# Adding the two terms of the rounded weights in one 512-column matmul, in the block products that share an accumulator

## The chip, the cores and the metric

The kernel runs on one core of a Trainium2 chip. The metric is the device time of one execution in microseconds; lower is better. A core has PE (the matrix engine, whose weight loads are listed as PEld), DVE (the vector engine), ACT (the scalar engine), POOL and SP. Each takes its own instructions in the order in which they were issued, and waits on the others by semaphores.

## The reference, cut to what matters

One decoder layer over 512 positions of width 1024, in float32: an FFN, a mixer, a second FFN, and a final norm.

```python
def swiglu(x, w_gate, w_up, w_down):
    return (jax.nn.silu(x @ w_gate) * (x @ w_up)) @ w_down
...
x = x + 0.5 * swiglu(rmsnorm(x, ffn1_norm[l]), ffn1_wg[l], ffn1_wu[l], ffn1_wd[l])
x = x + hybrid_mixer(rmsnorm(x, mix_norm[l]), ...)
x = x + 0.5 * swiglu(rmsnorm(x, ffn2_norm[l]), ffn2_wg[l], ffn2_wu[l], ffn2_wd[l])
return rmsnorm(x, final_norm)
```

The change lies in `x @ w_gate` and `x @ w_up` of both FFNs (`D_MODEL` 1024, `D_FF` 2816, so 22 tiles of 128 output rows for each of the two matrices).

## The kernel before, in words

**Split operands.** Every float32 matrix is split into a rounded part and the rest (`wh` and `wl` for weights; ACT rounds, DVE subtracts), and a product is made of three matmuls: rounded weight by rounded data, rounded weight by the data's rest, and the weight's rest by rounded data.

**`ffn_up`.** The first tiles go through plain products (`direct`). From tile `f0` (6 in the first FFN, 4 in the second) on, two tiles n and n+1 of one matrix are computed together by block products: the two weight tiles, each cut into two halves of 512 columns (H), and the data, cut into two halves of 256 positions, form a 2 by 2 block matrix product, which is done with seven products in place of eight. Sums and differences of the data blocks are made once (`moving_operands`); a data block `m` is a tile of 512 columns whose left half (`lo`) holds the rounded 256 columns and whose right half (`hi`) holds their rest. The sums of weight blocks (`s1` to `s4`) are made partly by adding DMAs of POOL, partly on DVE (`add_weights`).

**A pass** is one pair of tiles of one matrix: even passes `w` are the gate, odd ones the up matrix (`o.j = w % 2`). There are 16 passes in the first FFN and 18 in the second. In `stream` the products of a pass stand in the order 1, 2, 4 (of the pass before), 6, 3 (of the pass before), 5, 7. In the first pass there is no pass before, so its order is 1, 2, 6, 5, 7; the last pass ends with 6, 5, 7, 3 (of the pass before), 4, 3.

**A product** (`products`) has four column blocks of three matmuls of 256 columns each: rounded weights by `m[:, lo]`, rounded weights by `m[:, hi]`, rest of the weights by `m[:, lo]`. All three add into the left half of one accumulator of 512 columns. Products 1, 6, 7 and 4 of a pass share one accumulator, `o.beta` (a tile `mm`), in that order: each is read before the next adds to it. Product 2 has its own (`o.p2`) and 5 and 3 share `o.gamma` (both tiles `aux`).

**Reading** (`results`). After 1, 6 and 7 ACT copies the left half of `beta` out, into `t1` or `t2` (tiles `tg` in even passes, `tu` in odd ones). After 4 ACT applies Silu straight from `beta` in an even pass, and in an odd pass DVE multiplies `beta` with the gate. DVE adds what came from `p2` and `gamma`.

**Order.** The stretch is scheduled by hand (`manual_schedule`): one turn of the loop issues the matmuls of product i, the results of product i-1, and `prepare(i + LEAD)` with LEAD = 4: the weight sums due, ACT's rounding `wh` and DVE's rest `wl` of the product four places ahead. The split weights have three buffers of two products each. With `i % 14 == 12` and `i // 14 < f0` a turn also splits one tile of the FFN's hidden values (`halve`: ACT `hh`, DVE `hl`) for the down projection.

Of the kernel before, what the change touches and what calls it, by code (L numbers as in the profile page):

```python
# [11 lines left out]
AF = mybir.ActivationFunctionType  # L12
# [5 lines left out]
KD = D // P  # L18
# [162 lines left out]
def hybrid_kernel(ctx, tc, xt, vec, w1u, w1d, wm, wki, wrg, watt, wrnn, wout, w2u, w2d, both):  # L181
    nc = tc.nc

    out = both[0].rearrange("(k p c) -> k p c", k=KD, p=P)
    turned_out = both[1].rearrange("(j p c) -> j p c", j=2, p=P)
    plan = Plan()
    V, A = plan.engine("DVE", nc.vector), plan.engine("ACT", nc.scalar)
    G, T = plan.engine("POOL", nc.gpsimd), plan.engine("PE", nc.tensor)
# [21 lines left out]
    def slot(dt=F32, name="s"):  # L210
        return plan.take("slot", big.tile([P, S], dt, tag="slot", name=nm(name)))

    def work(name="t", cols=S):
        return plan.take("tmp", tmp.tile([P, cols], F32, tag="tmp", name=nm(name)))

    def awork(name="a"):
        return patt.tile([P, S], F32, tag="att", name=nm(name))

    def psum(tag="mm"):
        return psp.tile([P, S], F32, tag=tag, name=nm(tag))  # L220
# [26 lines left out]
    def wload(src, cols):  # L247
        r, h, l = wtiles(cols)
        Q.dma_start(r, src)
        wsplit(r, h, l)  # L250
        return h, l
# [69 lines left out]
    lo, hi = slice(0, HS), slice(HS, S)  # L321
# [62 lines left out]
    def ffn_up(y, wu, n0, hs, g, waiting=(), given=()):  # L384
# [10 lines left out]
        ws = []  # L395
# [65 lines left out]
        w = count - 1  # L461
# [26 lines left out]
        def products(i):  # L488
            p, w = stream[i]
            o = ws[w]  # L490
            if p == 1:
                o.beta = psum("mm")
            elif p == 2:
                o.p2 = psum("aux")
            elif p == 5:
                o.gamma = psum("aux")
            acc_ = {2: lambda: o.p2, 5: lambda: o.gamma, 3: lambda: o.gamma}.get(p, lambda: o.beta)()[:, lo]
            h, l = (t[:, i % 2 * H:(i % 2 + 1) * H] for t in units[i // 2])
            starts, opens = p in (1, 2, 5), dict(skip_group_check=p not in (1, 2, 5))
            for j in range(KD // 2):  # L500
                c = slice(j * P, (j + 1) * P)
                m = moving[{1: "n11", 2: "b21", 6: "t2", 5: "t1", 7: "r", 4: "q", 3: "n22"}[p]][j]
                T.matmul(acc_, h[:, c], m[:, lo], start=starts and j == 0, stop=False, **opens)
                T.matmul(acc_, h[:, c], m[:, hi], start=False, stop=False, **opens)
                T.matmul(acc_, l[:, c], m[:, lo], start=False, stop=j == KD // 2 - 1, **opens)

        def results(i):
            p, w = stream[i]
            o = ws[w]
            if p == 1:  # L510
                o.t1, o.t2 = (work("tg"), work("tg")) if o.j == 0 else (awork("tu"), awork("tu"))
                A.activation(o.t1[:, lo], o.beta[:, lo], AF.Copy)
            elif p == 2:
                V.tensor_sub(o.t1[:, lo], o.p2[:, lo], o.t1[:, lo])
            elif p == 6:
                A.activation(o.t1[:, hi], o.beta[:, lo], AF.Copy)
            elif p == 7:
                A.activation(o.t2[:, hi], o.beta[:, lo], AF.Copy)
                V.tensor_add(o.t2[:, hi], o.gamma[:, lo], o.t2[:, hi])
                if o.j:  # L520
                    o.h2 = slot(F32, "h")
                    V.tensor_mul(o.h2[:, hi], o.t2[:, hi], ws[w - 1].t2[:, hi])
                else:
                    A.activation(o.t2[:, hi], o.t2[:, hi], AF.Silu)
            elif p == 4:
                if o.j:
                    V.tensor_mul(o.h2[:, lo], o.beta[:, lo], ws[w - 1].t2[:, lo])
                else:
                    A.activation(o.t2[:, lo], o.beta[:, lo], AF.Silu)
            elif p == 3:  # L530
                V.scalar_tensor_tensor(o.t1[:, hi], o.gamma[:, lo], -1.0, o.t1[:, hi], op0=ALU.mult, op1=ALU.subtract)
                if o.j:
                    o.h1 = slot(F32, "h")
                    V.tensor_mul(o.h1, o.t1, ws[w - 1].t1)
                    hs.extend((o.h1, o.h2))
                else:
                    A.activation(o.t1, o.t1, AF.Silu)

        with tc.manual_schedule(engines=ENGINES):
# [32 lines left out]
            for i in range(len(stream)):  # L572
                products(i)
                if i:
                    results(i - 1)
                else:
                    together(results_direct(len(direct) - 1))
                if i + LEAD < len(stream):
                    prepare(i + LEAD)
                else:  # L580
                    halve(hs, f0 + i + LEAD - len(stream))
                if i % 14 == 12 and i // 14 < f0:
                    halve(hs, i // 14)
                if i % 7 == 1 and len(ws) < count:
                    load_ = load(len(ws))
                next(load_, None)
            results(len(stream) - 1)

    def halve(hs, n):
# [45 lines left out]
    for k in range(KD):  # L635
        if k:
            Q.dma_start(x[k], xt[k])
        if k % CH == 0:
            c = slice(k * P, (k + CH) * P)
# [8 lines left out]
    def given(r):  # L648
        h, l = (wsp.tile([P, WMAX], F32R, tag=t, name=nm(t)) for t in ("wh", "wl"))
        wsplit(r, h, l)  # L650
        return h, l

    y = []
    for k in range(KD):
        y.append(norm_tile(k, V_G1, False))
        if k % CH == 0:
            c = slice(k * P, (k + CH) * P)
# [4 lines left out]
    pu, w = psum(), given(AH[0])  # L662
# [672 lines left out]
    po, ws = psum(), []  # L1335
    for a, b in CHUNKS:
        w = wload(w2d[n, :, a * P:b * P], (b - a) * P)
# [42 lines left out]
    o = []  # L1380
# [84 lines left out]
```

## Time and profile before

| | us |
|---|---|
| three runs: 1092.8, 1093.52, 1094.61; median | 1093.52 |
| the profiled execution, its own time | 1094.6 |
| span of the profiled execution, first to last instruction | 1092.5 |
| block products of the first FFN, in the trace | about 74 to 235 |
| block products of the second FFN, in the trace | about 781 to 961 |

The profile is of one execution. Times are microseconds unless marked ns. The page gives each engine's busy time and instructions, and the costliest groups of instructions as line, engine, operation, result and operands by their names in the program, shape, count, busy time, mean duration in ns and idle time before them. Since all engine calls go through one helper, they all show its line, L175; the names tell them apart. `mm<-cm,wh` is a matmul of data block and rounded weights into `mm`, `wl<-s,wh` the rest of a weight sum. The chain of waits follows the work that ended last, in order of time, as start, length, what and count. The table by stage gives each engine's busy time and instruction count in a stretch. The timelines give start, length, engine, operation and count, and in brackets how long the engine had been idle and who released it. DVE's and ACT's lengths include a tail over which the next operation can start already.

### The profile page before, as it was taken

Reading aid. Unit: us, or ns where it says so; the run is one execution under the profiler, and the core shown is the slowest. Engines: PE = TensorE matmul, PEld = TensorE weight load, DVE = VectorE, ACT = ScalarE, POOL = GpSimd, SP = SyncE. Lnnn points to the kernel's source line nnn. Section 1 sums busy time; section 2 is a strip of 40 time slices with the busy share of each in tenths; the row PEclk is TensorE's granted clock in tenths of the full one; section 3 lists DMA queues with packets and bytes.
Section 4 is the critical chain, followed back from the end, with each engine's and each line's share of the span. In section 5 each row is a group of like instructions: output and inputs, shape, how many; then the busy total and the mean of one; then the engine's idle time right before and its main releaser. Section 6 shows DMA issues by size and latency. Waiting matters only on the chain.

```text
span 1092.5 us, 16466 instructions
## 1 busy us (share of the span) xinstructions
PE 1081.0 (99%) x6210; PEld 950.2 (87%) x6210; DVE 761.8 (70%) x1374; ACT 605.1 (55%) x1102; POOL 93.9 (9%) x115
## 2 busy tenths in 40 slices
PE   9999999999999999999999999999999999999997
PEld 7889999998888777888888888888899999988887
DVE  6687877785333778998899867666877777773233
ACT  6565655573222558969785564345655555562222
POOL 0151111100000000000000000002511111000000
PEclk9999999999999999999999999999999999999999
DMA  7396777733333442223232213435977777443322
GB/s 271 72 249 191 186 167 191 169 106 89 105 89 103 116 136 75 79 95 100 71 104 77 78 29 88 134 96 133 243 175 190 191 163 188 116 124 88 106 73 77
DMA packets 60607, 140.22 MB, mean 128 GB/s; under 512 B 7152, under 2 KB 15472, under 8 KB 60528
## 3 DMA queue, kind: packets, MB, share of 16 engines
q1 hardware_dynamic: 45264, 116.31, 33.9%
q0 software_dynamic: 14976, 22.55, 13.6%
q8 instruction: 48, 0.79, 0.3%
q10 hardware_dynamic: 288, 0.31, 0.1%
q14 instruction: 31, 0.25, 0.1%
HBM read 130.24 MB, written 2.10 MB: 121 GB/s over the span
## 4 chain that ended last, share of the span: by engine, by line
PE 87%; DVE 6%; ACT 4%; DMA 2%; issue 1%; SPq 0%; DVEq 0%; ACTq 0%; POOLq 0%
PE mm L175 58%; PE aux L175 29%; DVE wl L175 2%; ACT wh L175 1%; DMA gr<-wrg 1%; DVE yl L175 1%; DMA cm<-cb 1%; ACT L175 1%; DVE yf L175 0%; DMA x<-xt 0%; DVE ca L175 0%; ACT rl L175 0%; DVE h L175 0%; DVE xc L175 0%; ACT yh L175 0%
## 5 line engine op out<-in xcount | busy, mean ns | idle before, releaser
L175 DVE TENSOR_TENSOR wl<-wr,wh 128x1024 fp32r<-128x1024 f32 (+3 forms) x204 | 194.4, 956 | 149.0 <-ACT wh L175 148.4
L175 ACT ACTIVATE wh<-wr 128x1024 fp32r<-128x1024 f32 (+4 forms) x206 | 171.1, 835 | 173.2 <-PE mm L175 73.8
L175 PE MATMUL mm<-cm,wh 128*128 128x256 f32 x1088 | 199.0, 283 | 0.0
L175 PEld LDWEIGHTS mm<-cm,wh 128*128 128x128 f32 x1088 | 169.8, 192 | 0.2
L175 PE MATMUL mm<-yh,wh 128*128 128x512 f32 (+1 forms) x416 | 164.9, 397 | 1.3 <-ACT yh L175 0.7
L175 PE MATMUL mm<-yl,wh 128*128 128x512 f32 (+1 forms) x416 | 163.2, 393 | 0.9 <-DVE yl L175 0.8
L175 PE MATMUL mm<-yh,wl 128*128 128x512 f32 x408 | 160.0, 392 | 0.0
L175 PE MATMUL mm<-cm,wl 128*128 128x256 f32 x544 | 153.9, 283 | 0.0
L175 PE MATMUL aux<-cm,wh 128*128 128x256 f32 x816 | 150.3, 283 | 0.1
L175 PEld LDWEIGHTS aux<-cm,wh 128*128 128x128 f32 x816 | 127.4, 192 | 0.3 <-DMA cm<-cb 0.3
L175 PE MATMUL aux<-cm,wl 128*128 128x256 f32 x408 | 115.5, 283 | 0.0
L175 DVE TENSOR_TENSOR wl<-s,wh 128x512 fp32r<-128x512 f32 x136 | 93.3, 687 | 23.4 <-ACT wh L175 21.6
L175 ACT ACTIVATE wh<-s 128x512 fp32r<-128x512 f32 x136 | 83.0, 623 | 39.0 <-DVE s L175 30.9
L175 PEld LDWEIGHTS mm<-cm,wl 128*128 128x128 f32 x544 | 104.4, 192 | 0.0
L175 PEld LDWEIGHTS mm<-yh,wh 128*128 128x128 f32 (+1 forms) x416 | 78.4, 189 | 19.5 <-ACT yh L175 1.9
L175 PEld LDWEIGHTS mm<-yl,wh 128*128 128x128 f32 (+1 forms) x416 | 78.0, 187 | 17.3 <-DVE yl L175 2.2
L175 PEld LDWEIGHTS mm<-yh,wl 128*128 128x128 f32 x408 | 76.9, 189 | 16.6 <-DVE wl L175 0.3
L175 PE MATMUL mm<-hh,wh 128*128 128x512 f32 (+1 forms) x210 | 79.4, 378 | 0.0
L175 PE MATMUL mm<-hl,wh 128*128 128x512 f32 (+1 forms) x210 | 79.3, 377 | 0.0
L175 PE MATMUL mm<-hh,wl 128*128 128x512 f32 (+1 forms) x210 | 79.1, 377 | 0.0
L175 PEld LDWEIGHTS aux<-cm,wl 128*128 128x128 f32 x408 | 78.3, 192 | 0.0
L175 PE MATMUL aux<-hh,wh 128*128 128x512 f32 x154 | 59.9, 389 | 0.0
(220 smaller groups left out, 1898.6 us busy)
## 6 DMA issues: line engine op xcount, KB each, us to landing
wr<-wm SPq DMA_DIRECT2D x39, 512.0 KB, 3.6
wr<-w2u SPq DMA_DIRECT2D x26, 512.0 KB, 3.9
wr<-w1u SPq DMA_DIRECT2D x21, 512.0 KB, 5.5
s<-w2u SPq DMA_DIRECT2D x36, 256.0 KB, 4.7
s<-w2u POOLq DMA_DIRECT2D x36, 256.0 KB, 5.1
s<-w1u SPq DMA_DIRECT2D x32, 256.0 KB, 5.8
s<-w1u POOLq DMA_DIRECT2D x32, 256.0 KB, 5.5
wr<-w1d SPq DMA_DIRECT2D x16, 448.0 KB, 3.3
```

What stands on the lines that cost most here:

```text
L175: return call(*args, **kw)
```

## The change

In the products that go into `beta`, the two matmuls of the rounded weights, by `m[:, lo]` and by `m[:, hi]`, become one matmul of 512 columns, by the whole of `m`, into the whole accumulator: its left half takes the first term and its right half the second. The third matmul adds into the left half as before. In the last column block the order is turned, so that the wide matmul is last. When the accumulator is read, `whole` copies the right half with ACT and then adds the left half to the copy with DVE. Where ACT (Silu) or DVE (the product with the gate) read `beta` directly after product 4, `whole` now comes first, into `t2`. Products 2, 5 and 3 are as before.

```diff
-            acc_ = {2: lambda: o.p2, 5: lambda: o.gamma, 3: lambda: o.gamma}.get(p, lambda: o.beta)()[:, lo]
+            acc_ = {2: lambda: o.p2, 5: lambda: o.gamma, 3: lambda: o.gamma}.get(p, lambda: o.beta)()
...
-                T.matmul(acc_, h[:, c], m[:, lo], start=starts and j == 0, stop=False, **opens)
-                T.matmul(acc_, h[:, c], m[:, hi], start=False, stop=False, **opens)
-                T.matmul(acc_, l[:, c], m[:, lo], start=False, stop=j == KD // 2 - 1, **opens)
+                if acc_ is o.beta:
+
+                    wide = lambda: T.matmul(acc_, h[:, c], m, start=starts and j == 0, stop=j == KD // 2 - 1, **opens)
+                    rest = lambda: T.matmul(acc_[:, lo], l[:, c], m[:, lo], start=False, stop=False, **opens)
+                    for half in (wide, rest) if j < KD // 2 - 1 else (rest, wide):
+                        half()
+                    continue
+                T.matmul(acc_[:, lo], h[:, c], m[:, lo], start=starts and j == 0, stop=False, **opens)
+                T.matmul(acc_[:, lo], h[:, c], m[:, hi], start=False, stop=False, **opens)
+                T.matmul(acc_[:, lo], l[:, c], m[:, lo], start=False, stop=j == KD // 2 - 1, **opens)
+
+        def whole(out, acc_):
+            A.activation(out, acc_[:, hi], AF.Copy)
+            V.tensor_add(out, acc_[:, lo], out)
...
-                A.activation(o.t1[:, lo], o.beta[:, lo], AF.Copy)
+                whole(o.t1[:, lo], o.beta)
...
-                A.activation(o.t1[:, hi], o.beta[:, lo], AF.Copy)
+                whole(o.t1[:, hi], o.beta)
             elif p == 7:
-                A.activation(o.t2[:, hi], o.beta[:, lo], AF.Copy)
+                whole(o.t2[:, hi], o.beta)
                 V.tensor_add(o.t2[:, hi], o.gamma[:, lo], o.t2[:, hi])
...
             elif p == 4:
+                whole(o.t2[:, lo], o.beta)
                 if o.j:
-                    V.tensor_mul(o.h2[:, lo], o.beta[:, lo], ws[w - 1].t2[:, lo])
+                    V.tensor_mul(o.h2[:, lo], o.t2[:, lo], ws[w - 1].t2[:, lo])
                 else:
-                    A.activation(o.t2[:, lo], o.beta[:, lo], AF.Silu)
+                    A.activation(o.t2[:, lo], o.t2[:, lo], AF.Silu)
```

## The prediction

> **What bounds the kernel now.** I read the page first, then the chain of waits in order of time, then the table by stage, then the timelines of DVE and ACT. The page:
>
> ```profile
> span 1092.5 us, 16466 instructions
> PE 1081.0 (99%) x6210; PEld 950.2 (87%) x6210; DVE 761.8 (70%) x1374; ACT 605.1 (55%) x1102; POOL 93.9 (9%) x115
> L175 PE MATMUL mm<-cm,wh 128*128 128x256 f32 x1088 | 199.0, 283 | 0.0
> ```
>
> PE is at work for 99% of the span, and the matmuls that the change touches have no idle time ahead of them. Their 283 ns overlap, so the price of one is read from the chain, where the piece lengths are start to start:
>
> ```profile
> 173.66 1.44 PE aux L175 x12
> 175.10 2.88 PE mm L175 x24
> ...
> 280.48 14.96 PE aux L175 x66
> ```
>
> Twelve 256-column matmuls take 1.44 us: 120.0 ns each, and a block product 1.44 us. Sixty-six 512-column ones take 14.96 us: 226.7 ns each. The third view is a stage: one pair of passes (14 products, 20.16 us) in the first FFN.
>
> ```profile
> core 0: us, PE busy (x) PEld busy (x) DVE busy (x) ACT busy (x) POOL busy (x), PEclk, DMA share, GB/s
> 177.86:198.02 20.16, 20.16 (x170) 20.16 (x170) 15.52 (x28) 11.64 (x24) 3.50 (x4) 1.00 0.78 195
> ```
>
> PE sets the pace and DVE, with 28 operations and 15.52 us, looks as if it had 4.6 us to spare. How much of that is real depends on the waits inside it, so I need the timeline of DVE in that pair:
>
> ```profile
> 180.01 0.69 DVE L175 TENSOR_TENSOR h<-tu,tg 128x512 f32<-128x512 f32 x1
> ...
> 183.03 0.42 DVE L175 TENSOR_TENSOR tg<-aux,tg 128x256 f32<-128x256 f32 x1
> 184.45 1.48 DVE L175 TENSOR_TENSOR wl<-s,wh 128x512 fp32r<-128x512 f32 x2 [1.00 <-ACT wh L175]
> ...
> 187.59 0.69 DVE L175 TENSOR_TENSOR wl<-wr,wh 128x512 fp32r<-128x512 f32 x1 [0.73 <-ACT wh L175]
> ...
> 189.64 0.42 DVE L175 SCALAR_TENSOR_TENSOR tg<-aux,tg 128x256 f32<-128x256 f32 x1
> 189.97 0.68 DVE L175 TENSOR_TENSOR s<-s,wr 128x512 f32<-128x512 f32 x1
> 191.28 0.69 DVE L175 TENSOR_TENSOR wl<-a,wh 128x512 fp32r<-128x512 f32 x1 [0.62 <-ACT wh L175]
> ...
> 193.09 0.42 DVE L175 TENSOR_TENSOR tu<-aux,tu 128x256 f32<-128x256 f32 x1
> 193.54 0.43 DVE L175 TENSOR_TENSOR h<-tu,tg 128x256 f32<-128x256 f32 x1
> 193.88 0.69 DVE L175 TENSOR_TENSOR wl<-s,wh 128x512 fp32r<-128x512 f32 x1
> 194.49 0.69 DVE L175 TENSOR_TENSOR hl<-h,hh 128x512 fp32r<-128x512 f32 x1
> ```
>
> and the two places of ACT behind its waits:
>
> ```profile
> 183.48 0.42 ACT L175 ACTIVATE tg<-tg 128x256 f32<-128x256 f32 x1 [0.76 <-DVE tg L175]
> 183.80 0.61 ACT L175 ACTIVATE wh<-s 128x512 fp32r<-128x512 f32 x1
> ...
> 186.66 0.38 ACT L175 ACTIVATE tg<-mm 128x256 f32<-128x256 f32 x1 [0.93 <-PE mm L175]
> 186.94 0.62 ACT L175 ACTIVATE wh<-wr 128x512 fp32r<-128x512 f32 x1
> ```
>
> From these rows DVE has four prices. A 512-column step: from 180.01 to 183.03 there are five, 0.604 each. A 256-column step: 193.54 to 193.88, 0.33 to 0.34. The same step when the next operation reads its result: 193.09 to 193.54, 0.45. And a hand-off over ACT, when a DVE result goes to Silu, behind which the next rounding `wh` is queued, on which DVE's next `wl` waits: 183.03 to 184.45, 1.42, that is 1.09 over the step itself.
>
> **The matmuls.** The accumulator `beta` takes 4 of a pass's 7 products, each of four column blocks. In each block two matmuls of 256 columns (240.0 ns) become one of 512 (226.7): 13.3 ns saved. With 34 passes (16 and 18) that is 544 times, 7.25 us, or 0.43 us in a pair, whose PE time falls from 20.16 to 19.73. A page differs: the Trainium skill, "TensorE: Matmul & The Clock Gate", section "Wait — 56ns, not 53.3ns?", gives a warm matmul a fixed cost of about 2.5 ns over its columns. By that rule the whole saving would be an estimated 544 x 2.5 ns = 1.4 us. The trace speaks against it here (120.0 and 226.7 ns for 256 and 512 columns leave a fixed 13.3), so I keep 7.25.
>
> **The halves to be added.** `whole` copies the upper half on ACT and adds the lower one on DVE, for four products of a pass. The copy replaces one that was there, except for product 4, where it is new: 34 copies more on ACT and 136 additions more on DVE. The nearest rows:
>
> ```profile
> L175 DVE TENSOR_TENSOR h<-mm,tg 128x256 f32<-128x256 f32 x17 | 7.2, 424 | 1.1 <-PE mm L175 0.8
> L175 ACT ACTIVATE tu<-mm 128x256 f32<-128x256 f32 x51 | 19.2, 377 | 20.0 <-PE mm L175 20.0
> ```
>
> The same kind of operands, 424 ns, so a step of 0.33 (0.45 where the next operation reads it). ACT, busy 11.64 of 20.16, hides its copy.
>
> DVE's own loop over a pair, if PE never held it up: 20 steps of 512 (14 `wl`, 4 `s`, one `h`, one `hl`) at 0.604, 12.08; 8 of 256, 2.64; two of these read at once by the next, 0.24; one hand-off through the gate's Silu behind product 7, 1.09; the other Silu, 189.64 to 191.28, 1.64 with a step of 0.33 and one of 0.60 inside, so 0.71. Sum 16.76, 3.4 less than PE's time. The change adds 8 steps (2.64), three of them read at once by the next (0.36), and a second hand-off: product 4 of an even pass goes straight from `beta` to Silu today (186.66); now DVE's addition stands in front, so ACT's Silu and the `wh` behind it wait for DVE as at 183.03, 1.09. Together 4.09: **20.85 us for DVE against 19.73 for PE**. The average busy time hid that: a hand-off is idle time that nothing else fills, since DVE takes its operations in order.
>
> **Why PE then waits.** Product 6 adds into the bank that product 1's reader has to leave, and 7 and 4 follow likewise. The reader was ACT, alone; now DVE must have made its addition. From the end of product 1, PE has products 2 and 4 as cover, 2.83 us. In the DVE queue the addition stands behind the `wl` of a product four places ahead, so DVE's lag lands on PE. Release to PE costs little:
>
> ```profile
> 8.22 0.76 DVE yl L175
> 8.98 0.04 issue
> 9.03 12.57 PE mm L175 x54
> ```
>
> Once the lag has grown to 2.83 us PE runs at DVE's 20.85. Only pairs in which `halve` adds its `hl` (194.49) have that sum, by its condition (`i // 14 < f0`, 6 and 4) six in the first FFN and four in the second; the others are 0.60 shorter, 20.25. Against 20.16 before: +0.7 in 8 pairs (5.6; the first pair of each FFN has still to build the lag, and keeps its gain, -0.9) and +0.1 in 7 pairs (0.7).
>
> **The two ends of each stream.** In the first pass only one product lies between 1 and 6. The timelines of DVE and of PE there, in both FFNs:
>
> ```profile
> 77.12 0.68 DVE L175 TENSOR_TENSOR wl<-s,wh 128x512 fp32r<-128x512 f32 x1
> 77.72 0.69 DVE L175 TENSOR_TENSOR wl<-wr,wh 128x512 fp32r<-128x512 f32 x1
> 783.60 0.68 DVE L175 TENSOR_TENSOR wl<-wr,wh 128x512 fp32r<-128x512 f32 x1
> ```
>
> ```profile
> 76.93 0.50 PE L175 MATMUL mm<-cm,wh 128*128 128x256 f32 x2
> 783.66 0.39 PE L175 MATMUL mm<-cm,wh 128*128 128x256 f32 x2
> ```
>
> The addition goes between those two `wl`: 77.72 to 78.14, and product 6, which began at 76.93, at 78.18: 1.25 late. In the second FFN 783.60 to 784.02, so 784.06 for 783.66: 0.4. In the last pass product 7 follows 6 after one product. From the addition of 1 to that of 6, DVE has 0.33 + 0.60 + 0.60 + 0.33 + 0.60 + 0.33 + the hand-off with an `s` inside (1.09) + 0.60 = 4.5, PE 2.83 of cover: up to 1.65 late, of which I take 1.4, since PE itself comes a little late there; twice, 2.8.
>
> **Sum.** 5.6 - 0.9 + 0.7 + 1.65 + 2.8 = 9.9. The steps read 0.60 to 0.604 and 0.33 to 0.34, and where the lag shrinks in the seven short pairs PE gets a part of its 0.43 back; I take 9.0. The profiled execution took 1094.6 us (span 1092.5 and 2.1 around it), 1.1 above the median of 1093.5, so 1103.6 for a like execution, **1102.5** for the median. For the range: the hand-offs fully hidden and the others (rival one) at the lower end; each new addition at 0.45 instead of 0.33 at the upper.
>
> **Rivals.** *DVE keeps up*, and it ends faster: at product 4 the Silu and the `wh` behind it are early enough not to hold DVE. Then the loop is 19.76 in long pairs, PE's time, and 19.16 in short ones. The gain of 7.25 shows, less 1.65 and some 1.0 at the ends: -4.6, a median of 1089. For it: ACT is idle 42% of that stage. Against it: the 0.73 at 187.59 shows DVE waiting on that same `wh` already. It decides at the point where a loop falls under 19.73. Chance 0.12. *A draw*: half of that hand-off is hidden, the loops are 20.3 and 19.7; +1 or so, 1094. Chance 0.12. *All additions at the dependent price*: 0.12 more for the other five of a pair, 0.6 in 15 pairs, 9 us more: 1111. Chance 0.12. *The wide matmul saves nothing*: the weights are loaded once less, but 512 columns could cost 240 ns between 256-column ones, which no row shows mixed. As DVE sets the pace this costs only the first pairs' 0.9: 1103.5. Chance 0.05. My forecast keeps 0.59.
>
> A measurement of this kernel can tell about 0.2%, 2.2 us, from no change. Faster by more: 0.12; within: 0.12; slower: 0.76. The range of 1092.5 to 1109 leaves out the first rival and most of the third.
>
> **What would show it.** In the profile after: `mm<-cm,wh` at 128x512 x544 with some 227 ns a piece in the chain; PE matmuls on `mm` that wait for DVE `tg` and `tu`, some 34 times, 0.2 to 0.9 us each, at product 6; pairs of about 20.8 and 20.2 us instead of 20.16; DVE without idle but at the hand-offs, with over 18 us busy in a pair. It is wrong if PE shows no such waits, or if the pairs are 19.73.

## The result and the profile after

The changed kernel takes 1105.23 us (median of four runs, 1104.55 to 1105.73), the kernel before 1093.72: a ratio of 1.0105, interval 1.0087 to 1.0122, or 11.5 us slower. The forecast was 1102.5, from 1092.5 to 1109. The profiled execution took 1104.55 us.

The page of the kernel after, the lines that answer to those shown of before:

```profile
span 1102.8 us, 15526 instructions
PE 1083.1 (98%) x5666; PEld 919.0 (83%) x5666; DVE 805.0 (73%) x1510; ACT 610.8 (55%) x1136; POOL 93.9 (9%) x115
L175 PE MATMUL mm<-cm,wh 128*128 128x512 f32 x544 | 200.1, 403 | 8.0 <-DVE tg L175 5.3
```

544 matmuls are gone, and ahead of the 544 wide ones there are now 8.0 us of idle time, where there were 0.0. The view of waits, of PE alone (who waits for whom: us in total, times, longest):

```profile
PE mm L175 <- DVE tg L175: 5.3, 9, 1.1
PE mm L175 <- DVE tu L175: 2.6, 2, 1.3
```

Nine and two waits stand there; those of the odd passes, of a tenth of a microsecond each, are too short for it. One of the nine, in the timeline of PE:

```profile
179.15 0.40 PE L175 MATMUL mm<-cm,wh 128*128 128x512 f32 x1
180.07 0.49 PE L175 MATMUL mm<-cm,wh 128*128 128x512 f32 x1 [0.52 <-DVE tg L175]
180.40 0.28 PE L175 MATMUL mm<-cm,wl 128*128 128x256 f32 x1
180.52 0.40 PE L175 MATMUL mm<-cm,wh 128*128 128x512 f32 x1
180.75 0.28 PE L175 MATMUL mm<-cm,wl 128*128 128x256 f32 x1
```

At 179.15 the last matmul of product 4 begins, at 180.07 product 6. From 180.52 on a wide matmul holds PE for 0.23 us, so without a wait product 6 would have begun at 179.38: it is 0.69 us late. The table by stage, one long pair (with a `hl`) and one short pair:

```profile
179.25:200.10 20.85, 20.33 (x138) 18.39 (x136) 18.05 (x37) 11.89 (x26) 3.52 (x4) 1.00 0.72 178
890.30:910.60 20.30, 20.30 (x139) 18.39 (x137) 17.50 (x36) 11.44 (x25) 3.51 (x4) 1.00 0.72 172
```

DVE is busy 18.05 us of a long pair, where it was 15.52. What the other 2.8 us of the pair (20.85 - 18.05) are is shown by its timeline, over the same pair:

```profile
179.60 0.42 DVE L175 TENSOR_TENSOR tg<-mm,tg 128x256 f32<-128x256 f32 x1
179.93 0.68 DVE L175 TENSOR_TENSOR wl<-s,wh 128x512 fp32r<-128x512 f32 x1
...
187.26 0.41 DVE L175 TENSOR_TENSOR tg<-mm,tg 128x256 f32<-128x256 f32 x1
187.71 0.42 DVE L175 TENSOR_TENSOR tg<-aux,tg 128x256 f32<-128x256 f32 x1
189.14 0.69 DVE L175 TENSOR_TENSOR wl<-s,wh 128x512 fp32r<-128x512 f32 x1 [1.00 <-ACT wh L175]
...
191.61 0.41 DVE L175 TENSOR_TENSOR tg<-mm,tg 128x256 f32<-128x256 f32 x1
193.03 0.69 DVE L175 TENSOR_TENSOR wl<-wr,wh 128x512 fp32r<-128x512 f32 x1 [1.01 <-ACT wh L175]
...
194.58 0.42 DVE L175 SCALAR_TENSOR_TENSOR tg<-aux,tg 128x256 f32<-128x256 f32 x1
194.91 0.68 DVE L175 TENSOR_TENSOR s<-s,wr 128x512 f32<-128x512 f32 x1
196.21 0.69 DVE L175 TENSOR_TENSOR wl<-a,wh 128x512 fp32r<-128x512 f32 x1 [0.62 <-ACT wh L175]
...
199.88 0.68 DVE L175 TENSOR_TENSOR hl<-h,hh 128x512 fp32r<-128x512 f32 x1
200.49 0.42 DVE L175 TENSOR_TENSOR tg<-mm,tg 128x256 f32<-128x256 f32 x1
```

From the addition of product 1 (179.60, on which PE's 180.07 waits) to the next of its kind (200.49) it is 20.89 us. Between them DVE stops three times, each time for ACT's `wh`: at 189.14 (behind product 7), at 193.03 (behind product 4, new) and at 196.21 (behind 3). The middle one, in ACT's timeline:

```profile
190.32 0.37 ACT L175 ACTIVATE tg<-mm 128x256 f32<-128x256 f32 x1
192.06 0.42 ACT L175 ACTIVATE tg<-tg 128x256 f32<-128x256 f32 x1 [1.38 <-DVE tg L175]
192.39 0.61 ACT L175 ACTIVATE wh<-wr 128x512 fp32r<-128x512 f32 x1
```

ACT has copied its half by 190.69 and waits until 192.06 for DVE's addition (191.61 to 192.02); then come Silu, `wh`, and DVE's `wl` at 193.03.

### The profile page after: what moved, and what is told of

Same layout as the page of the kernel before. It is cut to its first block, busy times and chain, and to the rows that moved or that the text cites. A ratio compares the mean times of both kernels' runs of the same rounds, so it can differ in the third digit from the quotient of the medians.

```text
span 1102.8 us, 15526 instructions
## 1 busy us (share of the span) xinstructions
PE 1083.1 (98%) x5666; PEld 919.0 (83%) x5666; DVE 805.0 (73%) x1510; ACT 610.8 (55%) x1136; POOL 93.9 (9%) x115
## 4 chain that ended last, share of the span: by engine, by line
PE 75%; DVE 15%; ACT 4%; issue 3%; DMA 2%; SPq 0%; DVEq 0%; ACTq 0%
PE mm L175 52%; PE aux L175 24%; DVE wl L175 6%; ACT wh L175 3%; DVE tg L175 2%; DVE s L175 2%; DVE tu L175 1%; DVE h L175 1%; DMA gr<-wrg 1%; DVE yl L175 1%; DVE yf L175 0%; DVE hl L175 0%; DMA wr<-w1u 0%; DVE ca L175 0%; DMA x<-xt 0%
## 5 line engine op out<-in xcount | busy, mean ns | idle before, releaser
L175 PE MATMUL mm<-cm,wh 128*128 128x512 f32 x544 | 200.1, 403 | 8.0 <-DVE tg L175 5.3
L175 PEld LDWEIGHTS aux<-cm,wh 128*128 128x128 f32 x816 | 131.2, 190 | 3.9 <-DMA cm<-cb 0.4
L175 PE MATMUL mm<-cm,wl 128*128 128x256 f32 x544 | 130.7, 281 | 0.0
L175 PEld LDWEIGHTS mm<-cm,wh 128*128 128x128 f32 x544 | 100.0, 188 | 29.2 <-DVE tg L175 10.3
L175 ACT ACTIVATE tg<-tg 128x256 f32<-128x256 f32 (+1 forms) x61 | 31.2, 512 | 67.6 <-DVE tg L175 67.5
```

The source lines that it names most:

```text
L175: return call(*args, **kw)
```

## The experiments

Two theories stood against each other. The first: a loop of DVE and ACT sets the pace of the block products, made of 8 additions and a hand-off more in a pair, and PE waits for it at product 6. The rivals: the wide matmul saves nothing or costs time itself; DVE's additions alone are too much, whatever the order. All runs are given beside runs of the kernel before on the same chip. "Streams" are the two stretches of block products, from the start of the first to the start of the last of their matmuls in the timeline of PE: 161.60 and 181.32 us before, 167.84 and 185.78 after, together 10.7 us longer. The whole span grew by 10.3.

**The wide matmul alone.** The results are read as in the kernel before.

```diff
-            whole(o.t1[:, lo], o.beta)
+            A.activation(o.t1[:, lo], o.beta[:, lo], AF.Copy)
... (and so in products 6, 7 and 4)
```

> The wide matmul as in the change, but the accumulator is read as in the kernel before: ACT or DVE reads its left half alone, and the right half (the rounded weights by the data's rest, in four of seven products) is left out of the result. Theory (DVE's loop sets the pace, the wide matmul saves 13.3 ns of PE each): DVE is back at 16.8 us a pair, PE at 19.73, so no waits on DVE and the full 544 x 13.3 ns: 1093.7 - 7.2 = 1086.5 us, ratio to before 0.993. Rival (the wide matmul saves nothing, 512 columns between narrow ones cost 240 ns): 1093.7 us, pairs of 20.16 us.

Measured: 1087.68 us against 1093.25, ratio 0.9951 (0.9938 to 0.9963); streams 159.33 and 178.67. So the wide matmul does save: 5.6 us by the medians, 4.9 us in the two streams (338.0 instead of 342.9). Both are less than 7.2. The chain of waits of this run, in order of time:

```profile
103.33 2.81 PE mm L175 x16
106.15 2.88 PE aux L175 x24
...
123.20 2.82 PE mm L175 x16
```

Two products for the shared accumulator take 2.815 us, 352 ns for a wide and a narrow matmul, where the forecast had 226.7 + 120.0 = 346.7 and three narrow ones had 360. A pair is 123.20 - 103.33 = 19.87 us, not 19.73.

**The additions alone.** Three narrow matmuls, of which the one by `m[:, hi]` goes to the right half.

```diff
-                    wide = lambda: T.matmul(acc_, h[:, c], m, ...)
+                    T.matmul(acc_[:, lo], h[:, c], m[:, lo], ...)
+                    T.matmul(acc_[:, lo], l[:, c], m[:, lo], ...)
+                    T.matmul(acc_[:, hi], h[:, c], m[:, hi], ...)
```

> The opposite part alone: three matmuls of 256 columns as before, but the data's rest goes to the right half of the accumulator, so the halves are added when it is read, as in the change. Theory: DVE's loop is that of the change, 20.85 us in a long pair and 20.25 in a short one, and PE's own 20.16 lies under both, so the time is that of the change but for the few places where PE itself was the bound (some 1 us): 1105 to 1107 us. Rival one (the wide matmul, or its turned order in the last block, is what costs): 1094 to 1097 us. Rival two (PE's saving and the waits simply add up): 1105.2 + 7.2 = 1112.5 us.

Measured: 1105.25 us, ratio 1.0111 (1.0096 to 1.0127), streams 168.06 and 185.93; the change has 1.0105 and 167.84 and 185.78. With all of PE's saving taken away the time is the same. That is what it means that another engine sets the pace, and both rivals of this run fall: the wide matmul isn't what costs, and PE's saving and the waits don't add up. PE's waits in this run:

```profile
PE mm L175 <- DVE tg L175: 5.0, 10, 1.5
PE mm L175 <- DVE tu L175: 2.2, 2, 1.1
```

In sum they are a little less than in the change (5.3 and 2.6): PE's own matmuls take longer here (360 ns where the wide and the narrow one take 352), so it comes later and waits less for the same DVE.

**One Silu moved.** The Silu after product 4 is issued behind `prepare(i + LEAD)`.

```diff
-                    A.activation(o.t2[:, lo], o.t2[:, lo], AF.Silu)
+                    late.append(lambda: A.activation(o.t2[:, lo], o.t2[:, lo], AF.Silu))
...
+                while late:
+                    late.pop(0)()
```

> The change, with one instruction moved: the Silu after product 4 of an even pass is issued behind the rounding of the weights four places ahead, instead of ahead of it. Theory (the hand-off over ACT at product 4, 1.09 us of a pair, is part of the loop): long pairs fall from 20.87 to about PE's 19.8, short ones to 19.73; with starts and ends as they are, 1092 to 1095 us. Rival (the volume of DVE's work alone, 8 additions more in a pair, is what costs): no change, 1105 us.

Measured: 1096.36 us, ratio 1.0030 (1.0018 to 1.0041). Not one operation less on DVE, and most of the loss is gone, so it isn't the volume of DVE's work alone. But it is 1.4 us above the upper end of what I expected. The timeline of ACT, then of DVE:

```profile
168.68 0.42 ACT L175 ACTIVATE tg<-tg 128x256 f32<-128x256 f32 x1 [0.85 <-DVE tg L175]
169.00 0.37 ACT L175 ACTIVATE tu<-mm 128x256 f32<-128x256 f32 x1
169.27 0.62 ACT L175 ACTIVATE wh<-wr 128x512 fp32r<-128x512 f32 x1
```

```profile
165.75 0.69 DVE L175 TENSOR_TENSOR wl<-s,wh 128x512 fp32r<-128x512 f32 x1 [1.00 <-ACT wh L175]
...
168.56 0.68 DVE L175 TENSOR_TENSOR wl<-wr,wh 128x512 fp32r<-128x512 f32 x1
169.40 0.42 DVE L175 TENSOR_TENSOR tu<-mm,tu 128x256 f32<-128x256 f32 x1 [0.16 <-ACT tu L175]
169.92 0.69 DVE L175 TENSOR_TENSOR wl<-wr,wh 128x512 fp32r<-128x512 f32 x1
...
172.17 0.69 DVE L175 TENSOR_TENSOR wl<-a,wh 128x512 fp32r<-128x512 f32 x1 [0.62 <-ACT wh L175]
...
185.99 0.69 DVE L175 TENSOR_TENSOR wl<-s,wh 128x512 fp32r<-128x512 f32 x1 [1.00 <-ACT wh L175]
```

The late Silu still waits for DVE (0.85 idle), and now ACT's copy of the next product and its `wh` stand behind it. DVE's addition begins at 169.40 instead of 169.16 (0.60 after 168.56), its `wl` 0.52 after that instead of 0.33: 0.43 of the 1.09 came back. The loop is 185.99 - 165.75 = 20.24 us where the sum gave 20.85 - 1.09 = 19.76, still over PE's 19.87. The hand-offs behind products 7 and 3 are left (1.00 us idle at 165.75, 0.62 at 172.17).

**All three Silus moved,** in the same way.

> The change, with all three Silus of an even pass (after products 4, 7 and 3) issued behind the rounding of the weights four places ahead. Theory: the loop of DVE has no hand-offs left, 20.85 - 1.09 - 1.09 - 0.71 = 18.0 us in a long pair, under PE's 19.73, so pairs of 19.73 us and the gain of 7.2 us less the starts (1.5 us) and part of the ends (2.9 us): 1088 to 1091 us. Rival (volume of DVE's work): no better than with the one Silu moved.

Measured: 1090.26 us, ratio 0.9972 (0.9963 to 0.9982), 3 us under the kernel before; streams 160.59 and 179.24. The stage of one pair, and PE's waits for DVE in the whole run:

```profile
120.87:140.74 19.87, 19.87 (x138) 18.43 (x137) 18.56 (x38) 12.61 (x26) 3.51 (x4) 1.00 0.71 177
```

```profile
PE mm L175 <- DVE tg L175: 1.5, 2, 1.1
```

DVE is now busy 18.56 of 19.87 us, more than in the change, and PE has no idle time: the pair is as long as with the wide matmul alone. The two waits left are those at the start of each stream; the ones at the ends are gone as well.

**The control:** the same move in the kernel before.

> A control: the kernel before, with its three Silus of an even pass issued behind the rounding of the weights, as in the run with all three moved. Theory (before, PE sets the pace and DVE's loop of 16.8 us has slack, so hand-offs cost nothing there): no change, 1093.7 us, pairs of 20.16 us. Rival (moving the Silus is a gain of its own, and not the cure of the change's waits): 3 us or more faster than before.

Measured: 1093.74 us against 1094.02, ratio 1.0001 (0.9992 to 1.0010), streams 161.61 and 181.31. The move is worth nothing where PE sets the pace. It cures the change's waits and is no gain by itself.

**No hidden tiles split in the streams.**

```diff
-                if i % 14 == 12 and i // 14 < f0:
-                    halve(hs, i // 14)
```

> The change, without the splitting of hidden tiles during the block products; the tiles are split at the start of the down projection instead. Theory (DVE's loop): every pair becomes a short one, its period falls from 20.9 to 20.3 us, and the 0.7 us waits at product 6 of even passes go; in the two streams 8 x 0.6 = some 5 us less than in the change, part of it given back before the down projection, where 6 and 4 tiles must be split at once. Rival (the waits come from the hand-offs alone): pairs stay at 20.9 us.

Measured, in one run only: 1114.62 us; streams 164.32 and 183.44, 5.9 us less than in the change, as the loop demands, with pairs of 20.3. So the rival, pairs left at 20.9, falls. But 16 us came on top outside the streams (the span is 1112.8 against the change's 1102.8). In the waits of PE there are two new lines:

```profile
PE mm L175 <- ACT hh L175: 6.8, 2, 3.5
PE mm L175 <- DVE hl L175: 3.8, 2, 2.1
```

These are 10.6 us. About the rest shows in the granted clock of PE, which fell at the start of both down projections; the change has 1.00 there. In this table by stage it is the figure after POOL:

```profile
242.00:256.00 14.00, 12.31 (x45) 9.81 (x45) 12.37 (x37) 9.78 (x18) 0.00 (x0) 0.78 0.19 63
980.00:1000.00 20.00, 19.85 (x76) 16.18 (x77) 14.44 (x22) 10.59 (x18) 0.00 (x0) 0.86 0.16 46
```

A clock of 0.78 over 14 us and of 0.86 over 20 us is, by an estimate from these two rows, 3.1 + 2.8 = 5.9 us of PE's time. I had expected part of the gain to be given back; it was nearly three times the gain. The splitting has its place where it is.

**Wide and narrow matmuls grouped,** on top of the three moved Silus.

```diff
-                    for half in (wide, rest) if j < KD // 2 - 1 else (rest, wide):
+                    for half, k in ((wide, 0), (wide, 1), (wide, 2), (rest, 0), (rest, 1), (rest, 2), (rest, 3), (wide, 3)):
```

> The change with all three Silus moved, and in each product for the shared accumulator the matmuls ordered as three wide, four narrow, one wide, in place of wide and narrow in turn. In the run with the Silus moved a wide matmul takes 235 ns to the next start and a narrow one 118, where the plain products have 226.7 ns for 512 columns. Theory (the price comes from the change of width): wide behind wide falls to 227 ns, a product from 1.409 to about 1.39 us, 136 products: 2 to 3 us less, 1087.5 to 1088.5 us. Rival (a wide matmul with these operands costs 235 ns in any order): no change, 1090.3 us.

Measured: 1090.26 us, ratio 0.9961 (0.9949 to 0.9974); streams 160.36 and 179.01, 0.2 us less each. The mean distance from a wide matmul to the next start, over the timeline of PE, is 234 ns before another wide one of the same product and 228 before a narrow one. So neither theory holds as it stood: the order moves the price by a few ns, and does not bring it to 226.7. Why a wide matmul in these products takes 228 to 235 ns stays open. The 0.2 us are too little to show in the time.

**The first turn.** The preparation four places ahead is issued behind the first reading.

```diff
-                if i + LEAD < len(stream):
+                if i == 1:
+                    prepare(LEAD)
+                if i == 0:
+                    pass
+                elif i + LEAD < len(stream):
                     prepare(i + LEAD)
```

> The change with all three Silus moved, and in the first turn of each stream the rounding and the rest of the product four places ahead are issued one turn later, behind the first reading of the shared accumulator. Theory (the first wait of each stream, 1.3 and 0.5 us, is DVE's addition standing behind that rest): about 0.7 and 0.4 us less, 1089.2 us. Rival (that wait comes from the operands' DMA or from the end of the direct products): no change, 1090.3 us.

Measured: 1089.68 us, ratio 0.9958 (0.9946 to 0.9971). The interval overlaps with that of the run without this, so the time alone doesn't show the gain; the streams do: 159.96 and 178.67, shorter by 0.63 and 0.57, where 0.7 and 0.4 were expected. Of the waits for DVE, 1.1 us in the first stream and 0.3 in the second, 0.4 us in the first is left. So DVE's queue was the cause of most of it.

**The version that the runs point to.**

> The version that the runs point to: the change with all three Silus moved, the first turn's rounding one turn later, and the wide and narrow matmuls grouped. If the parts add up as the traces of the single runs show (1.2 us from the two starts, 0.4 us from the grouping, out of the streams of the run with the Silus moved): 1090.3 - 1.6 = 1088.7 us, some 5 us under the kernel before. If grouping is worth nothing, 1089.1 us.

Measured: 1088.86 us against 1093.11, ratio 0.9954 (0.9941 to 0.9968). The streams are 159.74 and 178.76, near those with no additions at all (159.33 and 178.67). Beside the run with the first turn alone (159.96 and 178.67) grouping adds no more than 0.1 us, and in the time the last three runs and the one with the three Silus moved can't clearly be told apart: their intervals overlap. The page:

```profile
span 1087.4 us, 15525 instructions
PE 1074.9 (99%) x5666; PEld 919.9 (85%) x5666; DVE 812.5 (75%) x1510; ACT 620.7 (57%) x1136; POOL 93.9 (9%) x115
```

PE, DVE, ACT and POOL have as many operations as in the change, and the span is 15 us shorter.

## Why the prediction was right, point by point

The places of the streams where time went, from the starts of product 2 of the same passes in both timelines of PE:

| Term | forecast, us | measured, us |
|---|---|---|
| first pass of each stream | 1.65 | 1.16 + 0.42 = 1.58 |
| first pairs | -0.9 | -0.1 |
| 8 long pairs | 5.6 | 3.63 + 2.17 = 5.80 |
| short pairs | 0.7 | 0.10 + 0.52 = 0.62 |
| last pass of each stream | 2.8 | 1.39 + 1.38 = 2.77 |
| both streams | 9.9, taken as 9.0 | 6.24 + 4.46 = 10.70 |

- *DVE's loop of 20.85 us in a long pair and 20.25 in a short one.* Shown: 20.89 in the timeline above, and 20.28 in a short pair, where product 6 of two odd passes, one pair apart, begins at 880.49 and 900.77. The three stops that the sum named are there with their size: 1.00, 1.01 and 0.62 us idle, and the timeline shows no other idle time of DVE in that pair. That the loop and not the matmul decides is shown by the run with the additions alone; that the hand-offs are its part that matters, by the runs with the Silus moved.
- *Product 6 as the place of the wait, some 34 times, 0.2 to 0.9 us.* Half right. Product 6 comes late in 30 of the 34 passes, and in the last pass of each stream product 7 does. But only in long pairs does product 6 of the even pass wait 0.7 us; in most other passes it is some 0.1 to 0.15, too short for the view of waits and less than the 0.2 named.
- *Starts and ends.* They came out to a tenth of a microsecond. For the first passes the walk from the two `wl` rows shows why: product 6 of the first pass, counted from the start of its stream, came 1.25 and 0.40 us later than before, as forecast. For the last passes the walk gave up to 1.65 each and the forecast took 1.4 without a row for the difference; that the measured ones are 1.39 and 1.38 is in part luck.
- *The matmul's saving.* Mis-sized: 226.7 ns came from products with 512 columns only, and beside narrow matmuls the wide one takes 235. The saving, where it could be seen, was 5.6 us (1093.25 - 1087.68), or 4.9 in the streams, instead of 7.25. The fixed cost that the Trainium skill gives in "TensorE: Matmul & The Clock Gate", section "Wait — 56ns, not 53.3ns?", would have made it an estimated 1.4. The run lies between, nearer to the rows. In the change itself this hardly counted, since PE waits anyway.
- *The first pairs.* Mis-sized: they gained 0.1 us instead of 0.9. Each took 20.12 us instead of 20.16. PE's own time there was 19.87 and not 19.73; and the other 0.25 us are waits, since product 6 came late in both of their passes already. That the lag had still to be built in the first pair was wrong.
- *From the sum to the time.* The forecast of 1102.5 was 2.7 us low. 0.9 of it is the step from the sum of 9.9 to 9.0, for which there was no row; 0.8 is the sum itself (10.7 measured in the streams), which is the first pairs; 0.8 lies between the streams' 10.7 and the medians' 11.5; and 0.2 is the median of before (1093.72 instead of 1093.5). What lies between 10.7 and 11.5 has no place in the traces: the profiled execution of before was the slowest of its four, that of after the fastest of its own, so the two profiles differ by 10.0 us (1104.55 - 1094.6) where the medians differ by 11.5.
- *The rivals.* "DVE keeps up" was not this kernel, but it named the right place: with the hand-offs out of the way DVE does keep up (18.56 of 19.87 us busy) and the time is 1090.3, where that rival had 1089. Its condition, that Silu and `wh` don't hold DVE, could be made true by an order. "A draw" needed half of the new hand-off hidden: DVE's 1.01 us idle at 193.03 show all of it. "All additions at the dependent price" is wrong: 179.60 to 179.93, 0.33 us, for one whose result the next operation doesn't read. "The wide matmul saves nothing" is wrong (0.9951).

## What to carry to other kernels

An engine that is busy three quarters of a stage need not have the last quarter to give: add up its own loop, with the steps at their start-to-start price and the stops where its next operation waits on an engine that waits on it, and compare that with the pace of the engine that leads. Here 4.1 us were added to a loop with 3.4 us of room, and a saving on the leading engine was lost with it. Before taking such a change back, look at the order: with the operation that waits issued behind the one that others wait for, the same additions fitted, and 11.5 us lost became 3 us won (with the first turn and the grouping 4, a step that the time alone can't tell from 3).

## What the runs showed of the hardware

- A 512-column matmul among 256-column ones takes 235 ns to the next start and the narrow one behind it 118, against 226.7 and 120.0 in products of one width; in groups of three it is 234 before another wide one and 228 before a narrow one. Why is open.
- After a wait the first wide matmul holds PE longer: 180.07 to 180.40, 0.33 us, against 0.23 for the next (180.52 to 180.75). All 32 waits for DVE in the change's block products have this extra tenth of a microsecond behind them (0.33 to 0.34 us). So has a narrow one behind a long wait in the run with the additions alone (0.22 instead of 0.12). The likely reason, which no run tests: in the timeline with the weight loads, the load for the matmul of 180.07 waits as well and begins at 180.07, where the load for that of 179.15 begins ahead of it, at 179.03.
- In the run without splitting in the streams, PE waits some 5 us in all at the start of each down projection, and its granted clock was 0.78 from 242 to 256 us and 0.86 from 980 to 1000; in the change, without these waits, it was 1.00 there. Why it fell no run tests.
